# A trunk layer on one core: w_up's right operands without their zero columns, first-half outputs written in two pieces, and the end of w_up in another order without GpSimd

## The chip, the core and the metric

The kernel runs on one core of a Trainium2 chip. The metric is the device time of one execution in microseconds (us), from the first to the last instruction with what the launch adds around them. Each kernel is run several times and the median counts. One further execution is recorded by the hardware profiler; rows and times within the kernel are from that one, counted from its first instruction.

## What is computed

One layer of a diffusion backbone for 128 context tokens and 512 latent tokens (640 in all), 1024 channels wide, in float32. Attention and a gated convolution are mixed, then follows a feed-forward part with a convolution over the tokens in its middle. The change lies in the feed-forward part:

```
def dwconv3(x, w):
    xp = jnp.pad(x, ((0, 0), (1, 1), (0, 0)))
    return w[0] * xp[:, :-2] + w[1] * xp[:, 1:-1] + w[2] * xp[:, 2:]

def conv_ffn(u, p):                       # u: (tokens, 1024), w_up: (1024, 2*2816), w_down: (2816, 1024)
    up = dwconv3(u @ p["w_up"], p["conv_ffn"])
    g, val = jnp.split(up, 2, axis=-1)
    return (jax.nn.silu(g) * val) @ p["w_down"]
```

Context and latent tokens are two separate sequences: the convolution sees a zero before the first and behind the last token of each.

## The kernel before, in words

**Products.** TensorE multiplies rounded operands (type fp32r). So that float32 accuracy is kept, each operand is cut in a high and a low part: ScalarE copies it to the rounded type (`hi_of`, line 1061, written as tile `whi`), VectorE subtracts that from the original (`lo_of`, line 1068, tile `wlo`). A product is three matmuls, high by high, high by low and low by high (`block`, line 1079, for w_up; `mm3`, lines 207 to 209, for w_down).

**w_up.** The 5632 columns of w_up are 44 blocks of 128: 22 blocks of g and 22 of val, the pair j being block j of each. One pair is a product of a 256 x 1024 matrix with the 1024 x 640 matrix u. The first two pairs (`NPLAIN` = 2) are computed plainly. The 20 others go through Winograd's form of Strassen's scheme with seven half-size products per pair (`strassen(j)`, line 1620): A11, A12, S2, S1, S3, S4, A22, each of 4 blocks of the inner dimension times three matmuls, 84 matmuls of 128 x 128 by 128 x `HALF`. The right operands are the quarters of u and sums of them, made once (tiles ZB0 to ZB2, ZT; `right_hi`, `right_lo`).

**The zero columns.** u is kept transposed, channels on partitions and tokens along the row, in two tiles UFa and UFb. A row has 644 columns (`NCOL`): a zero, 128 context tokens, a zero, 512 latent tokens, two zeros, so that the convolution can later read its neighbours from the product's row. Its halves, and so every matmul's moving operand in w_up, have 322 columns (`HALF`). GpSimd writes the zeros into UFa and UFb (six memsets, line 1381).

**Out of w_up.** A pair's sums come together in PSUM (two banks per pair, out of the ring 7, 0, 1) and are put into rows of a tile C: row `cg` of g, row `cv` of val. `copied` (line 1087, ScalarE, tiles p and u) takes a bank to SBUF; `added` (line 1090, VectorE) adds a bank to it and writes half a row of C; `last_copy` (line 1703, ScalarE) writes the last half. Three pairs later (`FLAG` = 3) the convolution runs on that row: `tap_mid` (line 1558, ScalarE) writes the middle tap into a row of tile Y, `taps_out` (line 1563, VectorE) adds the two outer taps to it, `silu` (1568, ScalarE), `gated` (1572, VectorE) multiplies g by val, `act_hi` (1578, ScalarE) and `act_lo` (1582) cut the result in ACTa and ACTb. Y has two pairs of rows; ACTa and ACTb have four slots.

**w_down.** Its first 512 output columns are summed within w_up's stage in banks 2 to 6, one block of 128 inner channels per pair (`down(k)`, line 1606, four pairs later), with weights in a tile WD of two blocks (`down_hi`, 1596, ScalarE; `down_lo`, 1600). The other 512 columns come behind w_up, with weights taken by `next_unit` (cut at lines 181 and 182) and the activations of the last four blocks straight from ACTa and ACTb (`again(i, ts)`, line 1932, i = 0 to 3 for k = 18 to 21); those of the 18 others were stored to memory and are fetched and cut again (`act_of`, tiles AFB, AHB, ALB).

**Order.** Each engine runs its instructions in the order in which the code issues them. Within `strassen(j)` that order is written out between the seven products. Behind the last pair stands a list by hand (lines 1942 to 1980) for w = 19, x = 20 and y = 21. TensorE's part of it is: `down(18)`, 15 matmuls of 512 columns; `again(0)` for two of the five token blocks, 6; `down(19)`, 15; the third block of `again(0)` and `again(1)`, 12; `down(20)`, 15; `again(2)`, 9; `down(21)`, 15; `again(3)`, 9; then the first half's sums are read out (`finish(0, t)`) and the other token blocks of `again` follow. With `late`, `down` runs all five token blocks with ACTa and WD's high part, then all with WD's low part, then all with ACTb (line 1618). At this end three low parts are GpSimd's: WD of `down(18)` and `down(19)` (within the last pair), ACTb of x, and one block of weights (`next_unit(G)`).

Of the kernel before, what the change touches and what calls it, by code (L numbers as in the profile page):

```python
# [11 lines left out]
F32 = mybir.dt.float32  # L12
F32R = mybir.dt.float32r
AF = mybir.ActivationFunctionType
# [3 lines left out]
D = 1024  # L18
KT = 8
NCTX = 128  # L20
# [5 lines left out]
DFF = 2816  # L26
NJ = DFF // 128
NCOL = 644
HALF = NCOL // 2
NACT = NCOL - 2  # L30
NRING = 4
FLAG = 3
# [75 lines left out]
def trunk_layer(ctx, tc, x_prompt, x_sample, cache_k, cache_v, c, c_ctx, w_ada, b_ada, g_pre1, g_post1, g_pre2,  # L108
# [1265 lines left out]
    TX = region(rb, "r4", [5, D], F32, "TX")  # L1374

    r7 = [rb.tile([128, n], F32, tag=f"r7{x}", name=f"UF{x}") for n, x in ((4 * NCOL, "a"), (3328, "b"))]
    UFS = [x[:, 0:4 * NCOL].rearrange("p (k c) -> p k c", c=NCOL) for x in r7]
    rows3 = r7[1][:, 4 * NCOL:4 * NCOL + 256].rearrange("p (i c) -> p i c", i=2)
    for a, b in ((0, 1), (NCTX + 1, NCTX + 2), (NCOL - 2, NCOL)):
        for x in UFS:  # L1380
            G.memset(x[:, :, a:b], 0.0)
# [89 lines left out]

    def modulated(t, hf):
        row = 1 if t == 0 else 0
        c0 = 1 if t == 0 else 2 + t * 128
# [33 lines left out]
    def crows(j):  # L1508
        if "c" not in room:
            room["c"] = region(ra, "r3", [7, NCOL], F32, "C")  # L1510
        return room["c"][:, j % 4, :], room["c"][:, 4 + j % 3, :]

    plain_out = {}

# [4 lines left out]
        block(plain_out[j, tok, i], (j, i), step, f"B{step + 1}{tok + 1}", step == 0, step == 1)  # L1519

    def plain_copy(j, tok, i):
        dst = crows(j)[i][:, tok * HALF:(tok + 1) * HALF]
        S.activation(dst, plain_out[j, tok, i], AF.Copy, scale=(1.0, -1.0)[i])

    def sums(j):

# [93 lines left out]
    def strassen(j):  # L1620

        f, nxt = j - FLAG, j + 1 if j + 1 < NJ else None
        g = NJ - FLAG if nxt is None else None
        cg, cv = crows(j)
        pair[j] = tuple(bank(n)[:, 0:HALF] for n in BANKS[j])
        if j > NPLAIN:
            last_copy(j - 1)
        else:
            plain_copy(1, 1, 1)
        if f >= 0:  # L1630
            tap_mid(f, 0)
        lo_of((j, 1))
        product(j, "A11")

        copied(j, "p1", 0)
        if f >= 0:
            tap_mid(f, 1)
            taps_out(f, 0, (0,))
        product(j, "A12")

        hi_of((j, 2), left(j, 2))
        added(cg[:, 0:HALF], j, "p1", 1)
        if f >= 0:
# [12 lines left out]
        if f >= 0:  # L1656
            gated(f)
        if nxt:
            adds = sums(nxt)
            adds[0]()  # L1660
        if g:
            cut_upto(len(state["cut"]) + 1)
            tap_mid(g, 0)
            tap_mid(g, 1)
        if j >= DLAG:
            down(j - DLAG)
        product(j, "S3")

        added(cv[:, HALF:], j, "p5", 0)
        lo_of((j, 3))  # L1670
        if nxt:
            pair_load(j + 2)
            hi_of((nxt, 0), left(nxt, 0))
            lo_of((nxt, 0))
            adds[1]()
        q = max((j - DLAG + 1) // 2, 0)
        if j == NPLAIN or (j > DLAG and (j - DLAG) % 2 == 1):
            down_hi(q)
            down_lo(q, G if g else V)
            down_load(q + 2 if q else 1)  # L1680
            if q == 0:
                down_load(2)
        if f >= 0:
            act_hi(f)
        if g:
            act_lo(f)
            taps_out(g, 0)
            silu(g)
        product(j, "S4")

        if nxt:
            hi_of((nxt, 1), left(nxt, 1))
        added(cg[:, HALF:], j, "u2", 1)
        if nxt:
            adds[2]()
        if g:
            taps_out(g, 1)
        elif f >= 0:
            act_lo(f)
        product(j, "A22")  # L1700

    def last_copy(j):
        S.activation(crows(j)[1][:, 0:HALF], pair[j][0], AF.Copy)


    for row in (1, 0):
# [61 lines left out]
    for t in range(1, NT + 1):  # L1768
        if t >= 2 and t != 4:
            normed(t - 2)  # L1770
        sq_b(t - 1)
        scaled(t - 1, 1)
        for k in (0, 1):
            if t < NT:
                wo_step(t, k)
        if t == NT:
            hi_of((1, 0), raws[1, 0])
            plain(0, 0, 0, 0)
        residual(t - 1)
# [12 lines left out]
        if t == 3:  # L1792
            right_hi("B11", "11", 0, 258)
            normed(2)
            right_lo("B11", "11", 0, 258)
        if t < NT:
            scaled(t, 0)
        if t == 3:
            right_hi("B21", "21", 0, 258)
        if t == 4:  # L1800
            right_hi("B11", "11", 258, HALF)
            right_lo("B11", "11", 258, HALF)
            right_lo("B21", "21", 0, 258)
            right_hi("B21", "21", 258, HALF)
            right_lo("B21", "21", 258, HALF)
        for k in range(3, KT):
            if t < NT:
                wo_step(t, k)
# [131 lines left out]
        bload(G2[:, row, :], 3, row)  # L1940
    w, x, y = NJ - 3, NJ - 2, NJ - 1
    us.append(state["cut"][state["next"]])
    gated(w)
    last_copy(y)
    act_hi(w)
    tap_mid(x, 0)
    down(NJ - 4)
    again(0, range(2))
    act_lo(w)
    tap_mid(x, 1)  # L1950
    taps_out(x, 0)
    tap_mid(y, 0)
    silu(x)
    taps_out(x, 1)
    tap_mid(y, 1)
    down(w, True)
    gated(x)
    down_hi(NJ // 2 - 1)
    act_hi(x)
    down_lo(NJ // 2 - 1)  # L1960
    act_lo(x, G)
    pms.append(bank(BANKS[NJ - 1][0]))
    again(0, (2,))
# [12 lines left out]
    down(y)  # L1976
    again(3, range(3))
    NU, tail, av = NJ // 2 - 2, 3, {}
    for t in range(NT):
# [47 lines left out]
```

## Time and profile before

| | us |
|---|---|
| median of 3 runs | 1115.15 (1114.73 to 1116.89) |
| the profiled execution, its own time | 1117.1 |
| its span, first to last instruction | 1115.3 |
| attention and what is ahead of the mixer's products | 0 to about 320 |
| the mixer's products by Strassen's scheme, 320 columns wide | about 320 to 555 |
| w_conv_out, w_o, second normalisation | about 555 to 669 |
| w_up, with half of w_down in it | 669.4 to 1013.5 |
| end of w_up: 96 matmuls from `down(18)` to `again(3)` | 1013.5 to 1040.7 |
| the rest of w_down | 1040.7 to 1109.0 |
| last residual and store | 1109.0 to 1115.3 |

How to read the views: "busy" of TensorE (PE) is modelled from pipelined matmuls, so matmul starts, not durations, tell its pace. A row of a timeline gives start, duration, engine, line, operation, operands as out<-in, and in brackets the idle time ahead of it with what ended it. PEclk is the TensorE clock that was granted, 1.00 being full speed.

### The profile page before, as it was taken

The page shows a single profiled execution, that of the slowest core. Times are in us where ns is not written, and L with a number is a line of the kernel's source. Part 1 is how long each engine was busy: PE and PEld are TensorE (multiplying, and loading weights), DVE is VectorE, ACT ScalarE, POOL GpSimd, SP SyncE. Part 2 cuts the span into 40 slices and gives each one's busy share as a digit, 9 for nine tenths or more (in the row PEclk, how much of TensorE's full clock was granted, in tenths as well). Part 3 has the DMA queues.
Part 4 walks back from the last instruction along what each step waited for, and adds up shares of the span by engine and source line. Part 5 has one row for each costly group of instructions (what it writes and reads, how often), then busy time and mean ns, then how long its engine had stood idle before and what let it go on. Part 6 is the DMA issues. An engine that isn't in the chain of part 4 may idle for free.

```text
span 1115.3 us, 20886 instructions
## 1 busy us (share of the span) xinstructions
PE 1082.4 (97%) x8581; PEld 999.5 (90%) x8581; DVE 815.6 (73%) x1211; ACT 567.5 (51%) x983; POOL 149.8 (13%) x194
## 2 busy tenths in 40 slices
PE   7999999988999999999999999999999999999997
PEld 5788877877999999999999889999999999997786
DVE  4578988785647889888555468888878877888544
ACT  5277677673335445454522365655546554555441
POOL 2056676640000000000000021000000000002001
PEclk9999999999999999999999999999999999999999
DMA  9683356341213223322332634333323332315722
GB/s 334 206 211 115 97 155 149 107 133 50 86 58 95 76 77 96 94 76 80 109 97 88 231 135 135 89 99 106 116 86 116 106 91 91 118 51 189 255 91 94
DMA packets 188989, 133.47 MB, mean 120 GB/s; under 512 B 16914, under 2 KB 171086, under 8 KB 188878
## 3 DMA queue, kind: packets, MB, share of 16 engines
q1 hardware_dynamic: 188782, 132.11, 39.1%
q8 instruction: 67, 1.10, 0.4%
q14 instruction: 28, 0.23, 0.1%
q10 hardware_dynamic: 112, 0.04, 0.0%
HBM read 120.01 MB, written 12.24 MB: 119 GB/s over the span
## 4 chain that ended last, share of the span: by engine, by line
PE 82%; DVE 7%; ACT 2%; issue 1%; POOL 0%; DVEq 0%; POOLq 0%; ACTq 0%
PE b L1079 46%; PE b L209 9%; PE b L207 9%; PE b L208 9%; PE s L852 2%; PE s L661 2%; DVE mx L804 1%; DVE PT L825 1%; DVE Y L1563 1%; PE s1b L852 1%; ACT pr L809 1%; PE s1a L207 1%; DVE PT L882 0%; PE s1b L207 0%; PE s1a L208 0%
## 5 line engine op out<-in xcount | busy, mean ns | idle before, releaser
L1079 PE MATMUL b<-ZB,whi 128*128 128x322 f32 x1024 | 228.5, 310 | 0.0
L1079 PEld LDWEIGHTS b<-ZB,whi 128*128 128x128 f32 x1024 | 173.8, 189 | 1.6
L1079 PE MATMUL b<-ZB,wlo 128*128 128x322 f32 x512 | 159.4, 311 | 0.0
L1079 PE MATMUL b<-MT,whi 128*128 128x320 f32 x608 | 134.1, 308 | 0.0
L1079 PEld LDWEIGHTS b<-MT,whi 128*128 128x128 f32 x608 | 101.6, 188 | 0.0
L1079 PEld LDWEIGHTS b<-ZB,wlo 128*128 128x128 f32 x512 | 96.2, 188 | 0.0
L1079 PE MATMUL b<-MT,wlo 128*128 128x320 f32 x304 | 93.8, 308 | 0.0
L1066 ACT ACTIVATE whi<-SUM 128x1024 fp32r<-128x1024 f32 x40 | 42.2, 1055 | 79.9 <-DVE SUM L1533 71.7
L1563 DVE SCALAR_TENSOR_TENSOR Y<-C,cffn,Y 128x642 f32<-128x642 f32 x88 | 81.0, 922 | 0.9
L182 DVE TENSOR_TENSOR wlo<-raw,whi 128x1024 fp32r<-128x1024 f32 (+1 forms) x31 | 33.6, 1085 | 53.3 <-ACT whi L181 52.8
L1079 PE MATMUL b<-UH,whi 128*128 128x320 f32 x228 | 70.5, 309 | 0.0
L1079 PE MATMUL b<-UL,whi 128*128 128x320 f32 x228 | 70.4, 309 | 0.0
L1079 PE MATMUL b<-UH,wlo 128*128 128x320 f32 x228 | 70.2, 308 | 0.0
L1070 DVE TENSOR_TENSOR wlo<-raw,whi 128x1024 fp32r<-128x1024 f32 (+1 forms) x51 | 50.4, 1020 | 25.3 <-ACT whi L1066 24.4
L1066 ACT ACTIVATE whi<-WB 128x1024 fp32r<-128x1024 f32 x38 | 40.1, 1056 | 54.9 <-DVE WB L1174 54.9
L1087 ACT ACTIVATE p<-b 128x322 f32<-128x322 f32 (+1 forms) x78 | 34.2, 439 | 57.9 <-PE b L1079 57.9
L1090 DVE TENSOR_TENSOR C<-b,p 128x322 f32<-128x322 f32 x40 | 19.7, 493 | 52.2 <-PE b L1079 51.8
L1079 PEld LDWEIGHTS b<-MT,wlo 128*128 128x128 f32 x304 | 57.0, 188 | 0.0
L1070 DVE TENSOR_TENSOR wlo<-WB,whi 128x1024 fp32r<-128x1024 f32 x38 | 46.5, 1223 | 8.9 <-ACT whi L1066 8.9
L1066 ACT ACTIVATE whi<-raw 128x1024 fp32r<-128x1024 f32 (+1 forms) x51 | 43.5, 892 | 18.2 <-PE b L209 9.8
L804 DVE TENSOR_REDUCE mx<-s 128x1 f32<-128x640 f32 x64 | 50.2, 811 | 3.3 <-PE s L661 3.0
L809 ACT ACTIVATE pr<-s,mx 128x640 f32<-128x640 f32 x56 | 44.1, 791 | 15.7 <-DVE mx L804 13.2
(400 smaller groups left out, 3096.8 us busy)
## 6 DMA issues: line engine op xcount, KB each, us to landing
raw<-in_w_in_dram SPq DMA_DIRECT2D x48, 512.0 KB, 3.8
RAW<-in_w_up_dram SPq DMA_DIRECT2D x40, 512.0 KB, 4.1
raw<-in_w_ada_dram SPq DMA_DIRECT2D x32, 512.0 KB, 4.4
raw<-in_w_down_dram SPq DMA_DIRECT2D x22, 512.0 KB, 3.9
actd<-Y SPq DMA_DIRECT2D x18, 321.0 KB, 2.6
AFB<-actd SPq DMA_DIRECT2D x18, 321.0 KB, 5.1
XT<-in_w_ada_dram SPq DMA_DIRECT2D x9, 512.0 KB, 5.9
raw<-in_w_conv_out_dram SPq DMA_DIRECT2D x9, 512.0 KB, 3.8
```

What stands on the lines that cost most here:

```text
L182: eng.tensor_tensor(out=lo[:, :n], in0=raw, in1=hi[:, :n].bitcast(F32), op=ALU.subtract)
L207: PE.matmul(out, ah, bh, start=start, stop=False)
L208: PE.matmul(out, ah, bl, start=False, stop=False)
L209: PE.matmul(out, al, bh, start=False, stop=stop)
L804: V.tensor_reduce(out=mx, in_=self.sc[h], axis=AX.X, op=ALU.max, negate=True)
L809: S.activation(self.pr[:, h, :], self.sc[h], AF.Exp, bias=mx, scale=rs, accum_out=self.sm[:, h:h + 1])
L852: PE.matmul(self.out(i, c % 2, 128, 384), VR[self.g][rows, c, :], PT[rows, s0:s0 + 4, :, 32 * c:32 * c + 32], start=n == 0, stop=n == 9, t ...
L1066: S.activation(to[0], raw, AF.Copy)
L1070: V.tensor_tensor(out=lo, in0=raw, in1=hi.bitcast(F32), op=ALU.subtract)
L1079: PE.matmul(out, p[:, ws], q[:, k, :], start=start and k == 0 and n == 0, stop=stop and k == 3 and n == 2, skip_group_check=True)
L1087: S.activation(t, pair[j][b], AF.Copy)
L1563: V.scalar_tensor_tensor(out=y, in0=crows(j)[i][:, d:d + NACT], scalar=cffn[:, 44 * d + o:44 * d + o + 1], in1=y, op0=ALU.mult, op1=ALU.add)
```

## The change

1. `HALF` is 320 in place of 322: u's rows hold the 640 tokens alone (`UFS`, `modulated`), and the six memsets on UFa and UFb go. Three memsets on C take their place, made once when C is first used (`crows`).
2. A row of C keeps its 644 columns with the zeros. Its first half now is tokens 0 to 319, which in C lie on either side of the zero between context and latent tokens: columns 1 to 128 and 130 to 321. So each write of a first half (`added` on `cg`, `last_copy` and `plain_copy`) becomes two instructions, of 128 and 192 columns (`into`, `filled`). The second half is one piece of 320.
3. In the last pair and behind it the order is new, and no low part is GpSimd's: WD, ACTb of x and the weights' low part go to VectorE. `down(y)` is `late` and comes ahead of `again(2)`. The outer taps of one row are issued apart (`taps_out(.., (0,))` and `(2,)`), with other work between them.

Not touched are the number of matmuls, the work on w_down's weights, and everything ahead of u's rows.

```
-HALF = NCOL // 2
+HALF = NTOK // 2
...
-    UFS = [x[:, 0:4 * NCOL].rearrange("p (k c) -> p k c", c=NCOL) for x in r7]
+    UFS = [x[:, 0:4 * NTOK].rearrange("p (k c) -> p k c", c=NTOK) for x in r7]
...
-    for a, b in ((0, 1), (NCTX + 1, NCTX + 2), (NCOL - 2, NCOL)):
-        for x in UFS:
-            G.memset(x[:, :, a:b], 0.0)
...
             room["c"] = region(ra, "r3", [7, NCOL], F32, "C")
+            for a, b in ((0, 1), (NCTX + 1, NCTX + 2), (NCOL - 2, NCOL)):
+                G.memset(room["c"][:, :, a:b], 0.0)
...
+    SIDES = (((0, NCTX, 1), (NCTX, HALF, 2)), ((0, HALF, HALF + 2),))
+
+    def into(row, side, f):
+        for a, b, c in SIDES[side]:
+            f(row[:, c + a:c + b], slice(a, b))
...
+    def filled(row, side, j, tag, b):
+        x = pair.pop((j, tag))
+        into(row, side, lambda dst, cs: V.tensor_tensor(out=dst, in0=pair[j][b][:, cs], in1=x[:, cs], op=ALU.add))
...
-        added(cg[:, 0:HALF], j, "p1", 1)
+        filled(cg, 0, j, "p1", 1)
...
-            down_lo(q, G if g else V)
+            down_lo(q)
...
+    tap_mid(x, 0)
     gated(w)
     last_copy(y)
+    taps_out(x, 0, (0,))
     act_hi(w)
-    tap_mid(x, 0)
+    tap_mid(x, 1)
     down(NJ - 4)
     again(0, range(2))
     act_lo(w)
-    tap_mid(x, 1)
-    taps_out(x, 0)
     tap_mid(y, 0)
+    taps_out(x, 0, (2,))
     silu(x)
     taps_out(x, 1)
     tap_mid(y, 1)
     down(w, True)
     gated(x)
+    act_hi(x)
+    taps_out(y, 0, (0,))
+    taps_out(y, 1, (0,))
     down_hi(NJ // 2 - 1)
-    act_hi(x)
     down_lo(NJ // 2 - 1)
-    act_lo(x, G)
+    taps_out(y, 0, (2,))
+    silu(y)
+    act_lo(x)
     pms.append(bank(BANKS[NJ - 1][0]))
     again(0, (2,))
-    next_unit(G)
-    taps_out(y, 0)
-    silu(y)
     again(1, range(3))
-    taps_out(y, 1)
+    taps_out(y, 1, (2,))
     down(x, True)
     gated(y)
+    next_unit()
     act_hi(y)
     act_lo(y)
     us.append(next_unit())
+    room["h"] = region(ra, "r3", [NT, D], F32, "HX")
+    down(y, True)
     again(2, range(3))
-    room["h"] = region(ra, "r3", [NT, D], F32, "HX")
-    down(y)
     again(3, range(3))
```

VectorE at the very end of w_up, before the change, from the last pair's sum of S4 (`C<-b,u`) on. Rows on Y from C are outer taps, `Y<-Y` is `gated`, ACTb is `act_lo`, WD is `down_lo`, L182 is the low part of weights:

```order
L1090 TENSOR_TENSOR C<-b_1223_10785,u_1227_10835 128x322
L1563 SCALAR_TENSOR_TENSOR Y<-C,cffn,Y 128x642 x2
L1572 TENSOR_TENSOR Y<-Y 128x642
L1582 TENSOR_TENSOR ACTb<-Y,ACTa 128x642
L1563 SCALAR_TENSOR_TENSOR Y<-C,cffn,Y 128x642 x4
L1572 TENSOR_TENSOR Y<-Y 128x642
L1600 TENSOR_TENSOR WD<-raw_10606,WD 128x1024
L1563 SCALAR_TENSOR_TENSOR Y<-C,cffn,Y 128x642 x4
L1572 TENSOR_TENSOR Y<-Y 128x642
L1582 TENSOR_TENSOR ACTb<-Y,ACTa 128x642
```

The same stretch of VectorE with the change, from x's last taps on:

```order
L1570 SCALAR_TENSOR_TENSOR Y<-C,cffn,Y 128x642 x3
L1579 TENSOR_TENSOR Y<-Y 128x642
L1570 SCALAR_TENSOR_TENSOR Y<-C,cffn,Y 128x642 x2
L1607 TENSOR_TENSOR WD<-raw_10642,WD 128x1024
L1570 SCALAR_TENSOR_TENSOR Y<-C,cffn,Y 128x642
L1589 TENSOR_TENSOR ACTb<-Y,ACTa 128x642
L1570 SCALAR_TENSOR_TENSOR Y<-C,cffn,Y 128x642
L1579 TENSOR_TENSOR Y<-Y 128x642
L182 TENSOR_TENSOR wlo_11075<-raw_10820,whi_11074 128x1024
L1589 TENSOR_TENSOR ACTb<-Y,ACTa 128x642
```

Two of y's four outer taps now stand ahead of WD's low part and two behind it; ACTb of x and the weights' low part, GpSimd's before, stand among them.

ScalarE at the same place before the change, from WD's high part for the last two blocks on (L1568 is `silu` of y, L181 weights' high parts, the ACTa rows are x's and y's):

```order
L1596 ACTIVATE WD<-raw_10606 128x1024
L1578 ACTIVATE ACTa<-Y 128x642
L181 ACTIVATE whi_11003<-raw_10782 128x1024
L1568 ACTIVATE Y<-Y 128x642
L1578 ACTIVATE ACTa<-Y 128x642
```

And with the change, from x's ACTa on:

```order
L1585 ACTIVATE ACTa<-Y 128x642
L1603 ACTIVATE WD<-raw_10642 128x1024
L1575 ACTIVATE Y<-Y 128x642
L181 ACTIVATE whi_11074<-raw_10820 128x1024
L1585 ACTIVATE ACTa<-Y 128x642
```

x's ACTa moved ahead of WD's high part, and y's `silu` ahead of the weights' high part.

TensorE behind `down(20)`, before the change (the first two rows are that block's last matmuls):

```order
L1618 MATMUL b_998_8393<-WD,ACTb 128x512
L1618 MATMUL b_999_8394<-WD,ACTb 128x512
L207 MATMUL b_1233_10934<-whi_11003,ACTa 128x512
L208 MATMUL b_1233_10934<-wlo_11004,ACTa 128x512
L209 MATMUL b_1233_10934<-whi_11003,ACTb 128x512
```

And with the change:

```order
L1625 MATMUL b_998_8399<-WD,ACTb 128x512
L1625 MATMUL b_999_8400<-WD,ACTb 128x512
L1625 MATMUL b_995_8396<-WD,ACTa 128x512
L1625 MATMUL b_996_8397<-WD,ACTa 128x512
L1625 MATMUL b_997_8398<-WD,ACTa 128x512
```

The nine matmuls of `again(2)` that stood between `down(20)` and `down(21)` now follow `down(21)`.

More of the change, by code (lines that the diff above doesn't have):

```diff
@@ L1521, in plain_copy @@
     def plain_copy(j, tok, i):
-        dst = crows(j)[i][:, tok * HALF:(tok + 1) * HALF]
-        S.activation(dst, plain_out[j, tok, i], AF.Copy, scale=(1.0, -1.0)[i])
+        into(crows(j)[i], tok, lambda dst, cs: S.activation(dst, plain_out[j, tok, i][:, cs], AF.Copy, scale=(1.0, -1.0)[i]))
+    def filled(row, side, j, tag, b):
+        x = pair.pop((j, tag))
+        into(row, side, lambda dst, cs: V.tensor_tensor(out=dst, in0=pair[j][b][:, cs], in1=x[:, cs], op=ALU.add))
     def sums(j):
@@ L1662, in strassen @@
             cut_upto(len(state["cut"]) + 1)
+            act_hi(f)
             tap_mid(g, 0)
-            tap_mid(g, 1)
+            act_lo(f)
+            taps_out(g, 0, (0,))
         if j >= DLAG:
@@ L1667, in strassen @@
         product(j, "S3")
-        added(cv[:, HALF:], j, "p5", 0)
+        filled(cv, 1, j, "p5", 0)
         lo_of((j, 3))
@@ L1682, in strassen @@
                 down_load(2)
-        if f >= 0:
+        if g:
+            tap_mid(g, 1)
+            taps_out(g, 0, (2,))
+            silu(g)
+            taps_out(g, 1, (0,))
+        elif f >= 0:
             act_hi(f)
[L1685 to L1688, printed above, removed]
         product(j, "S4")
@@ L1692, in strassen @@
             hi_of((nxt, 1), left(nxt, 1))
-        added(cg[:, HALF:], j, "u2", 1)
+        filled(cg, 1, j, "u2", 1)
         if nxt:
@@ L1696, in strassen @@
         if g:
-            taps_out(g, 1)
+            taps_out(g, 1, (2,))
         elif f >= 0:
@@ L1702, in last_copy @@
     def last_copy(j):
-        S.activation(crows(j)[1][:, 0:HALF], pair[j][0], AF.Copy)
+        into(crows(j)[1], 0, lambda dst, cs: S.activation(dst, pair[j][0][:, cs], AF.Copy))
     for row in (1, 0):
@@ L1792, in trunk_layer @@
         if t == 3:
-            right_hi("B11", "11", 0, 258)
+            right_hi("B11", "11", 0, 256)
             normed(2)
-            right_lo("B11", "11", 0, 258)
+            right_lo("B11", "11", 0, 256)
         if t < NT:
@@ L1798, in trunk_layer @@
         if t == 3:
-            right_hi("B21", "21", 0, 258)
+            right_hi("B21", "21", 0, 256)
         if t == 4:
[L1801 to L1805, printed above, removed]
+            right_hi("B11", "11", 256, HALF)
+            right_lo("B11", "11", 256, HALF)
+            right_lo("B21", "21", 0, 256)
+            right_hi("B21", "21", 256, HALF)
+            right_lo("B21", "21", 256, HALF)
         for k in range(3, KT):
```

2 lines of the change are left out of this document (1 added, 1 removed).

## The prediction

> **What bounds the kernel now.** I read the page first, then the chain of work that ended last, then starts.
>
> ```profile
> span 1115.3 us, 20886 instructions
> ...
> PE 1082.4 (97%) x8581; PEld 999.5 (90%) x8581; DVE 815.6 (73%) x1211; ACT 567.5 (51%) x983; POOL 149.8 (13%) x194
> ...
> PE 82%; DVE 7%; ACT 2%; issue 1%; POOL 0%; DVEq 0%; POOLq 0%; ACTq 0%
> ```
>
> TensorE carries the chain for 82% of the span. The busy times per stretch (columns PE, PEld, DVE, ACT, POOL, clock, DMA share, GB/s) say how sharply this holds in w_up:
>
> ```profile
> 736.00:1007.50 271.50, 271.50 (x1684) 260.09 (x1683) 222.31 (x280) 142.99 (x213) 0.00 (x0) 1.00 0.31 96
> ```
>
> In the steady pairs TensorE has no gap at full clock, VectorE is busy for 82% and ScalarE for 53%. So there only the pace of matmuls counts, and work added to the other two is free until it delays an operand. At the end of w_up this changes. The timeline of TensorE, start and duration first:
>
> ```profile
> 1007.52 0.46 PE L1079 MATMUL b<-ZB,whi 128*128 128x322 f32 x2
> ...
> 1011.88 0.42 PE L1079 MATMUL b<-ZT,wlo 128*128 128x322 f32 x1 [0.30 <-DVE wlo L1070]
> ...
> 1021.92 0.39 PE L207 MATMUL b<-whi,ACTa 128*128 128x512 f32 x1
> ...
> 1028.94 0.50 PE L208 MATMUL b<-wlo,ACTa 128*128 128x512 f32 x1 [0.33 <-POOL wlo L182]
> ...
> 1033.04 0.50 PE L207 MATMUL b<-WD,ACTa 128*128 128x512 f32 x1 [1.99 <-ACT ACTa L1578]
> ...
> 1035.12 0.63 PE L209 MATMUL b<-WD,ACTb 128*128 128x512 f32 x1
> ...
> 1040.68 0.39 PE L207 MATMUL b<-whi,ACTa 128*128 128x512 f32 x1
> ```
>
> Three waits stand here, the longest for ACTa of the last pair y. Behind it the clock falls:
>
> ```profile
> 1030.79:1034.20 3.41, 1.29 (x5) 0.59 (x4) 2.38 (x4) 1.69 (x2) 0.00 (x0) 1.00 0.54 147
> 1034.20:1037.62 3.42, 3.42 (x9) 2.65 (x9) 2.86 (x6) 2.52 (x6) 0.00 (x0) 0.50 1.01 401
> ```
>
> A stretch of 3.41 us in which TensorE was busy for 1.29 is followed by one at half clock.
>
> **The change, part by part: 320 columns.** The chain, in order of time (start, length, what), gives both paces:
>
> ```profile
> 369.92 185.09 PE b L1079 x1262
> ...
> 784.03 12.48 PE b L1079 x84
> 796.52 0.23 PE b L207
> ...
> 800.01 12.48 PE b L1079 x84
> ```
>
> The first row is the mixer, the same function with operands of 320 columns: 185.09 / 1262 = 146.7 ns per matmul. A pair in w_up: 12.48 / 84 = 148.6 ns with 322. The gap of 1.9 ns is more than the share of two columns, 148.6 x 2/322 = 0.9 ns. What the other 1.0 ns is the rows don't say; I take it that it goes with the row length, since function, engines and clock are the same, and VectorE is about as busy. w_up has 20 x 84 + 16 x 12 = 1872 such matmuls; the largest of their groups:
>
> ```profile
> L1079 PE MATMUL b<-ZB,whi 128*128 128x322 f32 x1024 | 228.5, 310 | 0.0
> ```
>
> Gain: 1872 x 1.9 ns = 3.6 us; lower end 1872 x 0.9 ns = 1.7 us; none would need 320 columns to run slower in w_up than in the mixer.
>
> The Trainium skill, "TensorE: Matmul & The Clock Gate", section "Wait — 56ns, not 53.3ns?", puts warm matmuls at N / 2.4 GHz plus 2.5 ns from start to start. Two columns would then be 0.83 ns and this term an estimated 1.6 us in place of 3.6; both measured paces lie some 11 ns above the rule, so I don't go by it.
>
> **Two pieces and memsets.** The groups of the steady pairs (736 to 1007), and ScalarE's and GpSimd's of the whole run (the numbers behind the bar: busy us, mean ns; then idle before):
>
> ```profile
> L1563 DVE SCALAR_TENSOR_TENSOR Y<-C,cffn,Y 128x642 f32<-128x642 f32 x68 | 60.1, 884 | 0.6
> L1090 DVE TENSOR_TENSOR C<-b,p 128x322 f32<-128x322 f32 x34 | 16.7, 493 | 47.0 <-PE b L1079 47.0
> L1572 DVE TENSOR_TENSOR Y<-Y 128x642 f32<-128x642 f32 x17 | 14.1, 829 | 1.8
> L1582 DVE TENSOR_TENSOR ACTb<-Y,ACTa 128x642 fp32r<-128x642 f32 x17 | 14.0, 823 | 0.0
> L1070 DVE TENSOR_TENSOR wlo<-RAW,whi 128x512 fp32r<-128x512 f32 x17 | 11.6, 681 | 0.0
> L1600 DVE TENSOR_TENSOR WD<-raw,WD 128x1024 fp32r<-128x1024 f32 x8 | 9.8, 1220 | 0.0
> ```
>
> ```profile
> L1578 ACT ACTIVATE ACTa<-Y 128x642 fp32r<-128x642 f32 x22 | 16.1, 734 | 5.2 <-DVE Y L1572 4.1
> L1596 ACT ACTIVATE WD<-raw 128x1024 fp32r<-128x1024 f32 x11 | 11.6, 1058 | 12.7 <-PE b L209 12.6
> L1703 ACT ACTIVATE C<-b 128x322 f32<-128x322 f32 x20 | 8.4, 422 | 0.0
> L1381 POOL MEMSET UFa<- 128x4 f32 x2 | 0.1, 106 | 333.2 <-issue 333.2
> ```
>
> From 512 to 1024 columns VectorE's subtraction rises by 539 ns, so about 140 ns of it do not depend on length. A second piece costs 0 to 0.14 us by that, at most a whole 0.49; I take 0.1 on VectorE, and on ScalarE 0 to 0.42 with 0.1 too. Per pair VectorE idles 47.0 / 17 = 2.8 us ahead of such additions, waiting for TensorE, and that hides it. The tightest follower is S1, which overwrites the bank that the two pieces read:
>
> ```profile
> 1000.75 0.49 DVE L1090 TENSOR_TENSOR C<-b,p 128x322 f32<-128x322 f32 x1 [0.64 <-PE b L1079]
> ```
>
> ```profile
> 1002.26 0.46 PE L1079 MATMUL b<-ZB,whi 128*128 128x322 f32 x2
> ```
>
> The addition ends at 1001.24, S1 starts at 1002.26: 1.0 us of cover. Behind the pieces on VectorE stand a tap and the low part for S3, which starts five microseconds later. Cost 0. The memsets, 0.1 us each, stand on an idle GpSimd, ahead of anything that reads C's zeros: 0.
>
> **The end.** From S3 of the last pair (1007.52) to the start behind `again(3)` (1040.68) 33.16 us pass. The 132 matmuls in it need 36 x 0.1486 + 96 x 0.2327 = 27.7 us, the latter pace being (800.01 - 796.52) / 15. So 5.5 us are lost to waits, restarts and half clock. What makes y late is seen on VectorE beside GpSimd:
>
> ```profile
> 1009.93 1.90 DVE L1070 TENSOR_TENSOR wlo<-RAW,whi 128x512 fp32r<-128x512 f32 x1
> ...
> 1024.41 6.88 DVE L1563 SCALAR_TENSOR_TENSOR Y<-C,cffn,Y 128x642 f32<-128x642 f32 x4
> ```
>
> ```profile
> 1008.85 2.43 POOL L1600 TENSOR_TENSOR WD<-raw,WD 128x1024 fp32r<-128x1024 f32 x1 [330.01 <-ACT WD L1596]
> 1024.21 1.73 POOL L1582 TENSOR_TENSOR ACTb<-Y,ACTa 128x642 fp32r<-128x642 f32 x1 [12.93 <-ACT ACTa L1578]
> 1025.90 2.98 POOL L182 TENSOR_TENSOR wlo<-raw,whi 128x1024 fp32r<-128x1024 f32 x1
> ```
>
> While GpSimd subtracts, 512 columns take VectorE 1.90 us in place of 0.68, and four taps 6.88 in place of 3.5. Without it VectorE saves 1.2 + 3.3 = 4.5 us and takes over WD (1.22), ACTb (0.82) and weights (1.22), of which only the first two stand ahead of y's ACTa, the weights after its gate.
>
> Now the new order from S3 on. S3 to A22 end at 1007.5 + 36 x 0.147 = 1012.8; A22's low part starts at 1009.9 and is there at 1010.6, before its first use at 1011.3, so the first wait goes. `down(18)` and six more run to 1017.7. VectorE meanwhile: WD 1.2, two taps 1.8, addition 0.5, tap 0.9, gate 0.8, from 1010.6 to 1015.8; ACTa of w by 1016.6, in time for `down(19)` at 1017.7. That ends at 1021.2. By then VectorE has done a tap, ACTb of w, three taps and x's gate (0.9 + 0.8 + 2.6 + 0.8, to 1021); y's first two taps follow (1.8, to 1022.7).
>
> From 1021.2 on two strings run side by side. TensorE: 12 + 15 matmuls, to 1027.5, then it needs y's ACTa. The others: WD's high part must wait until `down(19)` has read WD (0.2), then 1.06; WD's low part 1.22; tap 0.88; ACTb of x 0.82; tap 0.88; gate 0.83; ACTa 0.73: 6.6 us, to 1027.8; counted from 1022.7, when VectorE is free by the sums above, 1028.1. `again(2)`, 2.1 us of cover before, now stands behind. So a wait of 0.3 to 0.6 us is left, too short for the half clock, since 2.8 us of a stretch stay busy. I take 0.5 with 0.1 of restart. ACTb of y comes two instructions later (weights 1.22, then 0.82), at 1029.2, used 10 matmuls into `down(21)`, at 1030.3. `finish` of all blocks now waits for `down(21)`'s last five matmuls; `again(2)` and `again(3)`, 4.2 us, cover it. Gain 5.5 - 0.6 = **4.9 us**; at best 5.5.
>
> Sum: 3.6 + 4.9 = 8.5 us. The profiled execution (1117.1 with a span of 1115.3) would become 1108.6 with 1106.8. It stands 1.95 above the median of the three runs; I take the difference off the median: 1115.15 - 8.5 = 1106.65, said as **1106.7**.
>
> **Rivals.**
> - *Only two columns' worth* of pace: 1.7 in place of 3.6, so 1108.6. For it: nothing in the rows names the other 1.0 ns. Against it: 1262 matmuls of the mixer at 146.7. Chance 0.13. The rule above, 1.6 us, ends at much the same time.
> - *The wait for y stays long.* The two strings are near equal; if the second is later by 1.4 us, the wait is the 2 us of before and a half clock follows, 3.4 us at half pace, 1.7 lost. The end then gives 4.9 - 1.4 - 1.7 = 1.8, in all 5.4: 1109.8. It needs each of seven steps to be 0.2 us longer than its row says. Chance 0.10. The Trainium skill, same page, "Part 1: The HAM clock gate", has the clock fall after an idle window of about 3.4 us; here 2.1 idle of 3.41 were enough, so the row decides. By the rule this case would lose the wait alone.
> - *GpSimd isn't what slows VectorE* (the change doesn't do what it is said to): y's four taps keep their 3.3 us, all on the second string, and the half clock comes: the end gives 4.9 - 3.3 - 1.7 = -0.1, in all 3.5: 1111.7. Against it: the long instructions coincide with GpSimd's three. Chance 0.04.
> - *Slower:* the two pieces hold the bank and S1 waits in every pair. It begins where they end over 1.0 us later than one did; each further 0.1 us costs 20 x 0.1 = 2 us. To lose 2.2 us overall the pieces must take 0.49 + 1.0 + 0.54 = 2.0 us; at 2.2 us the time would be 1115.15 - 8.5 + 20 x 0.71 = 1120.9. The row of 0.49 speaks against it. Chance 0.03.
>
> **How the numbers follow.** Forecast 0.66, its own range 1105.9 to 1107.7 (no wait at all; a wait of 1.2). The remaining 0.04 are mixtures that leave less than 2.2 us. The range 1105.5 to 1110.0 takes in the first two rivals. About 0.2% (2.2 us) is what a measurement of this kernel can tell from no change: faster 0.93, same 0.04, slower 0.03.
>
> **What would show it.** Right: pairs of 84 matmuls in 12.32 us; no tap above 0.95 us in the last pairs; one wait of some 0.4 us ahead of `down(21)`; PEclk 1.00 until the last store. Wrong: 12.40 us per 84, a stretch at 0.50 behind 1027, or waits of TensorE for `C` within the pairs.

## The result, and the profile after

| | before | after |
|---|---|---|
| median, six runs each, before measured anew (us) | 1115.82 (1114.73 to 1118.29) | 1108.30 (1104.56 to 1109.73) |
| ratio | | 0.9924, 95% interval 0.9904 to 0.9945 |
| the profiled execution, its own time | 1117.1 | 1107.36 |
| its span | 1115.3 | 1105.6 |

The ratio is a gain of 8.5 us (6.1 to 10.7), which is what the prediction's sum gave; the median stands 1.6 us above the 1106.7 forecast, in the range. It also stands 0.6 us above the narrower range that the forecast's own mechanism was given (1105.9 to 1107.7) and next to the 1108.6 of the rival with two columns' share; the kernel before itself came out 0.7 us higher when measured anew, and between the two accounts the stages decide, not the median. The spread of 5 us among the runs follows the mean granted clock: the two shortest spans, 1102.8 and 1104.0 us, had 0.997, the two with 0.989 had 1107.6 and 1107.9.

The page of the changed kernel. TensorE does the same 8581 matmuls in 6.8 us less; its share of the chain of work is 83%, one point more.

```profile
span 1105.6 us, 20947 instructions
...
PE 1075.6 (97%) x8581; PEld 993.7 (90%) x8581; DVE 814.8 (74%) x1234; ACT 568.7 (51%) x1007; POOL 142.2 (13%) x188
...
PE 83%; DVE 5%; ACT 2%; issue 1%; POOL 0%; DVEq 0%; POOLq 0%; ACTq 0%
```

The chain in order of time (start, length, what): the mixer, and one of the pairs.

```profile
320.76 232.89 PE b L1079 x1596
...
797.54 12.31 PE b L1079 x84
```

A pair takes 12.31 us where it took 12.48: 146.5 ns a matmul, close to the 146.7 of the mixer before, as forecast (12.32). The mixer has changed too, which was not forecast; this is its row in the chain of before:

```profile
320.94 234.07 PE b L1079 x1596
```

In the steady pairs (same columns of the view as in the prediction) TensorE still has no gap and GpSimd no instruction; VectorE's share went from 82% to 83%:

```profile
731.00:1002.80 271.80, 271.80 (x1698) 259.70 (x1697) 225.98 (x301) 146.38 (x234) 0.00 (x0) 1.00 0.31 97
```

The groups of those pairs show the two pieces (mean ns behind the bar). 291 + 349 ns stand where one piece took 493, and VectorE still waits 4.8 us in 17 pairs ahead of the first piece and 38.3 us ahead of the other half's:

```profile
L1530 DVE TENSOR_TENSOR C<-b,p 128x320 f32<-128x320 f32 x17 | 8.4, 492 | 38.3 <-PE b L1079 38.3
L1530 DVE TENSOR_TENSOR C<-b,p 128x192 f32<-128x192 f32 x17 | 5.9, 349 | 0.0
L1530 DVE TENSOR_TENSOR C<-b,p 128x128 f32<-128x128 f32 x17 | 4.9, 291 | 4.8 <-PE b L1079 4.8
```

The end, TensorE's timeline from S3 of the last pair to the start behind `again(3)`:

```profile
1002.82 0.46 PE L1079 MATMUL b<-ZB,whi 128*128 128x320 f32 x2
...
1021.56 1.33 PE L1625 MATMUL b<-WD,ACTb 128*128 128x512 f32 x5
1023.07 2.59 PE L1625 MATMUL b<-WD,ACTa 128*128 128x512 f32 x10 [0.18 <-ACT ACTa L1585]
...
1030.83 0.39 PE L207 MATMUL b<-whi,ACTa 128*128 128x512 f32 x1
```

Of the three waits one is left. It stands in the bracket with 0.18 us; by the starts it is more, since five matmuls from 1021.56 at 0.2327 us would let the next start at 1022.72, and it starts at 1023.07, 0.35 us later. The stretches around it stay at full clock (the number behind POOL's count is PEclk):

```profile
1019.60:1023.00 3.40, 3.29 (x15) 2.30 (x13) 3.30 (x5) 2.42 (x4) 0.00 (x0) 1.00 0.72 173
1023.00:1026.40 3.40, 3.33 (x14) 2.74 (x15) 2.25 (x3) 1.44 (x3) 0.00 (x0) 1.00 0.94 359
1026.40:1029.80 3.40, 3.40 (x16) 2.76 (x15) 3.15 (x7) 3.40 (x11) 0.00 (x0) 1.00 1.03 413
```

VectorE there, without GpSimd beside it: 512 columns in 0.68 us where they took 1.90, WD's low part in 1.2, two taps in 1.68.

```profile
1005.18 0.68 DVE L1070 TENSOR_TENSOR wlo<-RAW,whi 128x512 fp32r<-128x512 f32 x1
1005.78 1.22 DVE L1607 TENSOR_TENSOR WD<-raw,WD 128x1024 fp32r<-128x1024 f32 x1
1006.92 1.68 DVE L1570 SCALAR_TENSOR_TENSOR Y<-C,cffn,Y 128x642 f32<-128x642 f32 x2
...
1017.75 1.23 DVE L1607 TENSOR_TENSOR WD<-raw,WD 128x1024 fp32r<-128x1024 f32 x1 [0.34 <-ACT WD L1603]
```

By these anchors the profiled executions differ like this (us):

| stage | before | after | change |
|---|---|---|---|
| start to the mixer's first product | 320.78 | 320.60 | -0.18 |
| mixer, first to last product | 233.92 | 232.75 | -1.17 |
| from there to S3 of the last pair (1007.52; 1002.82) | 452.82 | 449.47 | -3.35 |
| S3 to the start behind `again(3)` | 33.16 | 28.01 | -5.15 |
| from there to the end | 74.63 | 74.75 | +0.12 |
| span | 1115.31 | 1105.58 | -9.73 |

### The profile page after: what moved, and what is told of

It is laid out like the page before. It is cut to its first block, busy times and chain, and to the rows that moved or that the text cites. A ratio compares the mean times of both kernels' runs of the same rounds, so it can differ in the third digit from the quotient of the medians.

```text
span 1105.6 us, 20947 instructions
## 1 busy us (share of the span) xinstructions
PE 1075.6 (97%) x8581; PEld 993.7 (90%) x8581; DVE 814.8 (74%) x1234; ACT 568.7 (51%) x1007; POOL 142.2 (13%) x188
## 4 chain that ended last, share of the span: by engine, by line
PE 83%; DVE 5%; ACT 2%; issue 1%; POOL 0%; DVEq 0%; POOLq 0%; ACTq 0%
PE b L1079 45%; PE b L207 9%; PE b L209 9%; PE b L208 9%; PE s L852 3%; PE s L661 2%; DVE mx L804 1%; DVE PT L825 1%; ACT pr L809 1%; PE s1b L852 1%; PE b L1625 1%; PE s1a L207 1%; PE s1a L208 0%; PE s1a L209 0%; PE s1b L207 0%
## 5 line engine op out<-in xcount | busy, mean ns | idle before, releaser
L1079 PE MATMUL b<-ZB,whi 128*128 128x320 f32 x1024 | 225.9, 308 | 0.0
L1079 PE MATMUL b<-ZB,wlo 128*128 128x320 f32 x512 | 157.8, 308 | 0.0
L1570 DVE SCALAR_TENSOR_TENSOR Y<-C,cffn,Y 128x642 f32<-128x642 f32 x88 | 77.5, 884 | 0.7
L182 DVE TENSOR_TENSOR wlo<-raw,whi 128x1024 fp32r<-128x1024 f32 (+1 forms) x32 | 34.9, 1090 | 53.2 <-ACT whi L181 49.9
L1087 ACT ACTIVATE p<-b 128x320 f32<-128x320 f32 x78 | 34.1, 437 | 54.0 <-PE b L1079 52.2
L1530 DVE TENSOR_TENSOR C<-b,p 128x128 f32<-128x128 f32 (+2 forms) x60 | 20.9, 377 | 46.9 <-PE b L1079 46.0
```

What stands on the lines that cost most here:

```text
L182: eng.tensor_tensor(out=lo[:, :n], in0=raw, in1=hi[:, :n].bitcast(F32), op=ALU.subtract)
L1079: PE.matmul(out, p[:, ws], q[:, k, :], start=start and k == 0 and n == 0, stop=stop and k == 3 and n == 2, skip_group_check=True)
L1087: S.activation(t, pair[j][b], AF.Copy)
L1570: V.scalar_tensor_tensor(out=y, in0=crows(j)[i][:, d:d + NACT], scalar=cffn[:, 44 * d + o:44 * d + o + 1], in1=y, op0=ALU.mult, op1=ALU.add)
```

## The experiments

The short name **E** stands below for the time from S3 of the last pair to the start behind `again(3)`. A single run's time moves by some microseconds with the clock ahead of the mixer, so the stages are compared, and medians where several rounds were run.

**The two halves of the change, each alone.** The first kernel has part 1 and 2 (columns, pieces) with the order of before; the second has part 3 (order, no GpSimd) with 322 columns. The first, against the changed kernel:

```
-            down_lo(q)
+            down_lo(q, G if g else V)
...
-    act_lo(x)
+    act_lo(x, G)
...
+    next_unit(G)
+    taps_out(y, 0)
+    silu(y)
...
+    again(2, range(3))
...
-    down(y, True)
-    again(2, range(3))
+    down(y)
```

> The columns alone: 320 columns and the two pieces, with the old order at the end and GpSimd's three low parts. Theory (two separate terms): the pairs run at 146.6 ns per matmul, the stretch from the last pair's S3 to the matmul behind again(3) stays at 33.1 us, and the whole gains 3.6 us, ratio 0.9968. Rival (the columns alone make the end shorter too, because all that VectorE and ScalarE do there has two columns less): the stretch falls below 32 us and the gain is over 5 us. Rival (the pieces cost TensorE something): more than 146.9 ns, or waits for the bank ahead of S1.

The second, against the changed kernel:

```
-HALF = NTOK // 2
+HALF = NCOL // 2
...
-        filled(cg, 0, j, "p1", 1)
+        added(cg[:, 0:HALF], j, "p1", 1)
```

> The end alone: rows of 322 columns with zeros and one-piece writes as before, with the new order and no low part on GpSimd. Theory: 148.6 ns per matmul in the pairs, 28.1 us from S3 of the last pair to behind again(3) in place of 33.2, gain 5.0 us, ratio 0.9955. Rival (the end needs the shorter rows to come out even): over 29 us and a wait of over 1 us for y's ACTa.

The columns alone: 1112.39 against 1116.93, ratio 0.9959 (0.9945 to 0.9973), 146.55 ns a matmul in w_up, E 31.60. The order alone: 1112.0, ratio 0.9957 (0.994 to 0.9974), 148.61 ns, E 28.23 with no wait. So each half is worth about 4.7 us, and the product of the ratios, 0.9916, lies within the interval of the whole change, 0.9904 to 0.9945, as it should if they add. Of the first kernel's gain 1.2 us lie in the mixer (below), which its theory did not have. The first kernel keeps the three waits of before and the long taps:

```profile
1007.85 0.41 PE L1079 MATMUL b<-ZT,wlo 128*128 128x320 f32 x1 [0.36 <-DVE wlo L1070]
...
1024.88 0.50 PE L208 MATMUL b<-wlo,ACTa 128*128 128x512 f32 x1 [0.44 <-POOL wlo L182]
...
1029.00 0.50 PE L207 MATMUL b<-WD,ACTa 128*128 128x512 f32 x1 [1.99 <-ACT ACTa L1585]
```

Its longest wait is 1.99 us, the same as before the change; but the clock stays at 1.00 behind it, and E is 31.60 where it was 33.16. The theory's 33.1 did not hold; the rival's figure did, but not its reason, since the wait is no shorter and y's four taps are as long (6.87 us; 6.88 before). The stretch in question is read under the last pair of experiments.

**Which part of the end: order or GpSimd.** The changed kernel with the three low parts back on GpSimd:

```
-            down_lo(q)
+            down_lo(q, G if g else V)
...
-    act_lo(x)
+    act_lo(x, G)
...
-    next_unit()
+    next_unit(G)
```

> The changed kernel with its new order, but the same three low parts back on GpSimd (WD within the last pair, ACTb of x, the weights cut behind y's gate). Theory (GpSimd slows VectorE while both run): the 512-column subtraction takes 1.9 us again instead of 0.7, what VectorE runs beside ACTb of x is longer by 1 to 1.7 us, y's ACTa comes 0.5 to 1.5 us later, and the stretch from S3 to behind again(3) is 28.5 to 29.8 us, against 28.0. Rival (the order alone made the end short): 28.0 us, and no long instruction on VectorE.

The other corner, the order of before with all low parts on VectorE, is the kernel of columns alone with these three edits reversed.

> 320 columns and the old order, but the three low parts on VectorE. Theory (both count: without GpSimd y's four taps take 3.5 us again, but three low parts of 3.3 us in all now stand ahead of them): y's ACTa comes about 1 us earlier than in the old kernel, the wait ahead of down(21) is 0.5 to 1.5 us, no half clock, and the stretch from S3 to behind again(3) is 29 to 30.5 us. Rival (only GpSimd counts): 28.0 to 28.5 us. Rival (only the order counts): 33 us.

With the new order and GpSimd E is 28.41, 0.40 more than without and just below what the theory gave. With the old order and VectorE E is 30.03, as forecast. In the four corners, all at 320 columns:

| E (us) | low parts on GpSimd | on VectorE |
|---|---|---|
| old order | 31.60 | 30.03 |
| new order | 28.41 | 28.01 |

So the order is the larger part (2.0 to 3.2 us), and GpSimd costs 1.6 in the old order, 0.4 in the new. Which of the moves within the order counts was not tested. What the new order takes from GpSimd's harm is seen in the third kernel. Its VectorE, then its GpSimd:

```profile
1007.21 1.92 DVE L1070 TENSOR_TENSOR wlo<-RAW,whi 128x512 fp32r<-128x512 f32 x1
...
1020.49 1.58 DVE L1607 TENSOR_TENSOR WD<-raw,WD 128x1024 fp32r<-128x1024 f32 x1 [0.94 <-ACT WD L1603]
...
1025.40 2.35 DVE L1589 TENSOR_TENSOR ACTb<-Y,ACTa 128x642 fp32r<-128x642 f32 x1 [0.81 <-ACT ACTa L1585]
```

```profile
1006.18 2.40 POOL L1607 TENSOR_TENSOR WD<-raw,WD 128x1024 fp32r<-128x1024 f32 x1 [325.64 <-ACT WD L1603]
...
1018.81 2.17 POOL L1589 TENSOR_TENSOR ACTb<-Y,ACTa 128x642 fp32r<-128x642 f32 x1 [10.22 <-DMA G<-bct]
...
1024.66 2.40 POOL L182 TENSOR_TENSOR wlo<-raw,whi 128x1024 fp32r<-128x1024 f32 x1 [3.68 <-ACT whi L181]
```

VectorE's three are long exactly where GpSimd's three run, but y's taps stand between two of them (1.67 us for two), and the low part that the last one stretches is not needed until ten matmuls later. Only the first still costs a wait, 0.36 us ahead of A22; `down(21)` has none, although the theory had y's ACTa come 0.5 to 1.5 us later.

One more kernel gives GpSimd a single low part, the one that no matmul waited for:

```
-    act_lo(x)
+    act_lo(x, G)
```

> The changed kernel with ACTb of x alone given back to GpSimd, where it took 2.2 us with nothing of TensorE's waiting for it; WD and the weights' low part stay VectorE's. Theory (VectorE's string sets the wait of 0.35 us ahead of the last down): VectorE loses 0.82 us of that string, its taps beside GpSimd's 2.2 us grow by at most as much, the wait goes: 27.5 to 27.9 us from S3 of the last pair to the start behind again(3), in place of 28.0, and a median within 0.5 us of the changed kernel's, 0.992 of the time before. Rival (the shared port takes from VectorE what it saves): the wait grows to 0.8 to 1.5 us, 28.4 to 29.1 us there, 0.5 to 1 us more in all.

The ratio is 0.9924 (0.9906 to 0.9941), the changed kernel's own; E is 28.21, between the two forecasts. On VectorE WD's low part now takes 2.17 us, 0.94 more, while ACTb's 0.82 has left it:

```profile
1017.53 2.17 DVE L1607 TENSOR_TENSOR WD<-raw,WD 128x1024 fp32r<-128x1024 f32 x1 [0.34 <-ACT WD L1603]
```

```profile
1016.44 2.17 POOL L1589 TENSOR_TENSOR ACTb<-Y,ACTa 128x642 fp32r<-128x642 f32 x1 [338.14 <-PE b L1625]
```

The theory, that the string gets shorter, has fallen: the wait of 0.18 us in the brackets became 0.38. No kernel here was shown to be faster than the changed one.

**Why 322 columns cost 2.1 ns more.** Two kernels keep all else of the change. In one the rows stand 322 apart and 320 columns are read; in the other the rows stand 320 apart and 322 columns are read, two of them the next row's, whose sums nobody reads (so the length written to PSUM is 322 as well; the last row of a tile, one in 8 or 16, is read with 320).

```
-    ZB0 = ra.tile([128, 4, 4, HALF], F32R, tag="r0", name="ZB0")
+    ZB0 = ra.tile([128, 4, 4, 322], F32R, tag="r0", name="ZB0")
...
-        TT[i] = (z[:, a], z[:, a + 1])
+        TT[i] = (z[:, a, :, 0:HALF], z[:, a + 1, :, 0:HALF])
```

> The changed kernel with w_up's right operands still 320 columns long, but stored 322 columns apart (1288 bytes), as their rows were before. Theory (where a row starts sets the 1.0 ns beyond two columns' share): 147.6 ns per matmul in the pairs. Rival (the length of 322 sets it): 146.6 ns.

```
-                PE.matmul(out, p[:, ws], q[:, k, :], start=start and k == 0 and n == 0, stop=stop and k == 3 and n == 2,
+                    at = (row + 4 * (n == 1) + k) * HALF
+                    mv = flat[:, at:at + HALF + (2 if row + 4 * (n == 1) + k + 1 < rows else 0)]
+                    out = wide[:, 0:mv.shape[1]]
...
+                PE.matmul(out, p[:, ws], mv, start=start and k == 0 and n == 0, stop=stop and k == 3 and n == 2,
```

> The changed kernel with rows 320 columns apart, but the pairs' moving operands read 322 columns (two of the next row, whose products are not used; the last row of a tile, 4 of 84 matmuls, stays at 320). Theory (where a row starts): 147.5 ns per matmul, two columns' share of 0.9 ns alone. Rival (the length of 322): 148.5 ns.

A third is the second with 4 in place of the 2: 324 columns.

> The changed kernel with rows 320 apart, every w_up matmul of the seven products reading 324 columns (four of the next row's; the sums' four extra columns are not read, so the output stays). In question is why 322 columns cost 148.6 to 148.7 ns a matmul, 2.1 more than 320 (146.55), when 320 to 512 rises by (232.7 - 146.55) / 192 = 0.449 ns a column. Theory: the length counts in steps of four columns, so that 322 is paid like 324: here 146.55 + 4 x 0.449 = 148.3 to 148.7, the same as with 322. Rival: some fixed surcharge of 1.2 ns falls on every length that is no multiple of 64 or on every reading across a row's end: here 146.55 + 1.8 + 1.2 = 149.5.

The chains' rows of a pair, for these three in turn:

```profile
829.03 12.34 PE b L1079 x84
```

```profile
785.57 12.49 PE b L1087 x84
```

```profile
783.31 12.54 PE b L1087 x84
```

| columns read | rows apart | us per 84 | ns a matmul |
|---|---|---|---|
| 320 | 320 | 12.31 | 146.5 |
| 320 | 322 | 12.34 | 146.9 |
| 322 | 322 | 12.48 | 148.6 |
| 322 | 320 | 12.49 | 148.7 |
| 324 | 320 | 12.54 | 149.3 |

The length of the matmul makes the difference, not where rows start: the theory of the first kernel fell, the rival was right. Steps of four columns fell as well, since 324 is not paid like 322 (149.3, with 148.3 to 148.7 expected); nearer is the surcharge on top of the columns. By (232.7 - 146.55) / 192 = 0.449 ns a column, 322 would cost 147.45 and 324 148.35; 1.2 to 1.3 and 0.9 ns are left over. This takes the slope between 320 and 512 columns as even, which no run shows; what is left over is open.

**The mixer's 1.2 us.** In all kernels so far the mixer goes with the size of the tiles of u's quarters, made later in the same memory: 233.92 us with 322 (the kernel before, the order alone, rows 322 apart), 232.7 to 232.8 with 320. UH and UL, the high and the low part of the mixer's right operand, use the memory of the first and the second of these tiles. The largest difference lies in matmuls on UH with the weights' high part; their group in the mixer (window 321 to 553), before and after:

```profile
L1079 PE MATMUL b<-UH,whi 128*128 128x320 f32 x228 | 70.5, 309 | 0.0
```

```profile
L1079 PE MATMUL b<-UH,whi 128*128 128x320 f32 x227 | 69.1, 304 | 0.0
```

The mean of one fell from 309 to 304 ns; 228 x 5 ns = 1.1 us. (The expectations below give the same step from the start of such a matmul to the next one, on UL, as 147.1 and 142.1 ns. Rows of a timeline are rounded to 10 ns, so only the difference of some 5 ns counts.) Two kernels put 32 unused columns behind the first and behind the second of u's tiles:

```
-    ZB0 = ra.tile([128, 4, 4, HALF], F32R, tag="r0", name="ZB0")
+    ZB0 = ra.tile([128, 16 * HALF + 32], F32R, tag="r0", name="ZB0")[:, 0:16 * HALF].rearrange("p (a k c) -> p a k c", a=4, k=4)
```

> The changed kernel with 32 unused columns (128 bytes per partition) behind the first tile of u's quarters, which stands in the memory of the mixer's UH: so UL and all that is allocated behind it start 128 bytes later, as they did before the change; nothing else differs. Theory (where UL stands sets the pace of the mixer's matmuls that go from UH to UL): these matmuls go from 142.1 to 147.1 ns, the mixer from 232.75 to 233.9 us, w_up stays at 146.55. Rival (the two columns of every row, not the place, did it in some other way): all stays as in the changed kernel.

```
-    ZB1 = ra.tile([128, 4, 4, HALF], F32R, tag="r1", name="ZB1")
+    ZB1 = ra.tile([128, 16 * HALF + 32], F32R, tag="r1", name="ZB1")[:, 0:16 * HALF].rearrange("p (a k c) -> p a k c", a=4, k=4)
```

> The same 32 unused columns behind the second tile, which stands in the memory of UL: UH and UL stay where they are in the changed kernel, and what is allocated behind UL starts 128 bytes later. Theory (UL's place relative to UH counts): the mixer stays at 232.75 us and 142.1 ns. Rival (the place of something behind it counts, weights or sums of operands): 233.9 us and 147.1 ns, as before the change.

Both texts give the shift as 128 bytes; it is 64. The first tile's memory is as large as the largest tile that uses it: before the change u's tile of 16 rows of 322 columns, 20608 bytes per partition; after it AHB of w_down's rest, 8 rows of 642 columns or 20544 bytes, since u's tile is now smaller (20480). The 32 columns make it 20608 again. The same holds for the second tile's memory, with ALB. So with the first shift UL and all that is allocated behind it start 64 bytes later than in the changed kernel: UL where it was before the change, the tiles behind it still 64 bytes or more ahead of where they were. With the second, UL stays and all behind it starts 64 bytes later. Between these two kernels only UL's memory stands elsewhere.

Their mixers in the chain:

```profile
320.57 234.09 PE b L1079 x1596
```

```profile
321.32 233.63 PE b L1079 x1596
```

The first shift gives back all 1.2 us (233.95 from first to last product; that group's mean is 309 ns again) and 0.2 ns per matmul in w_up; the second, which leaves UH and UL in place, gives back 0.74 of them (233.49; 307 ns). So the place of tiles in memory does it, with nothing else changed: 64 bytes on all that stands behind UL are worth 0.74 us, the same on UL another 0.46. Neither theory covers the second. Which of the tiles behind UL count, and why a place counts, is open.

**How much wait the end bears.** Products of 1024 columns without use, on VectorE ahead of y's `gated`, delay y's ACTa; with two:

```
+    V.tensor_tensor(out=EX[:, 4, :], in0=G2[:, 0, :], in1=G2[:, 1, :], op=ALU.mult)
+    V.tensor_tensor(out=EX[:, 4, :], in0=G2[:, 0, :], in1=G2[:, 1, :], op=ALU.mult)
     gated(y)
```

> The changed kernel with two more VectorE products of 1024 columns (1.22 us each, their result is overwritten later) ahead of y's gate. Theory (the two strings behind down(19) are near equal, so y's delay goes straight to TensorE, and a wait of over half a clock stretch costs a half clock): a wait of 2.4 to 2.7 us ahead of down(21), one stretch of 3.41 us at half clock behind it unless the wait falls across two stretches, and 30.4 to 32.2 us from S3 to behind again(3). Rival (the clock falls only after a whole idle stretch of 3.41 us): the wait alone, 30.4 us. Rival (slack hides it): 28.0 us.

With one of the two lines:

> The changed kernel with one more VectorE product of 1024 columns (1.22 us, its result is overwritten later) ahead of y's gate. Theory: a wait of 1.2 to 1.5 us ahead of down(21), no half clock, and 29.2 us from S3 to behind again(3). Rival (any wait above 1 us costs a half clock): 30.9 us.

One makes the wait 1.12 us and E 28.95, 0.94 more than without. Two make it 2.38 and E 31.78, 2.83 more for the second: the wait's 1.26 and a stretch at half clock. The half clock came as expected, and E with two products; with one, E is 0.25 us shorter than expected, and both waits are a little shorter.

```profile
1024.60 2.59 PE L1625 MATMUL b<-WD,ACTa 128*128 128x512 f32 x10 [1.12 <-ACT ACTa L1585]
```

```profile
1025.60 4.15 PE L1625 MATMUL b<-WD,ACTa 128*128 128x512 f32 x10 [2.38 <-ACT ACTa L1585]
```

The stretch ahead of the half clock and the one in it, with two products:

```profile
1022.50:1025.91 3.41, 1.03 (x5) 0.53 (x4) 3.38 (x5) 1.10 (x2) 0.00 (x0) 1.00 0.91 296
1025.91:1029.33 3.42, 3.42 (x9) 2.67 (x8) 1.88 (x3) 0.59 (x1) 0.00 (x0) 0.50 1.02 413
```

And the kernel of columns alone, whose wait of 1.99 us was not followed by half clock:

```profile
1024.25:1027.66 3.41, 2.31 (x9) 1.43 (x8) 3.27 (x4) 0.74 (x1) 0.58 (x1) 1.00 0.00 0
1027.66:1031.08 3.42, 1.95 (x7) 1.33 (x8) 2.50 (x3) 2.36 (x4) 0.00 (x0) 1.00 0.83 249
```

These bounds are not free to choose. That kernel's half-clock stretches ahead of the mixer start at 85.59, 225.54 and 256.26 us: 41 and 9 times 3.413 us apart; the next one, behind its last matmul, starts at 1106.18, 299 steps of 3.4133 us from the first. Counted on by 276 such steps from the first, a bound falls at 1027.66, within the wait, which so is shared between two stretches, busy for 2.31 and 1.95 us. In the kernel before, whose half-clock stretches start at 85.30 and 1034.20, 278 steps apart, the same wait fell into one stretch, of which 1.29 us were busy. The same wait cost 1.5 us more in the one execution than in the other (33.16 - 31.60, less 36 x 2.0 ns for the columns). That the share decides is not shown sharply: ahead of the mixer a stretch busy for 1.94 of 3.41 us was followed by half clock (the changed kernel, from 169.62 us), and one busy for 1.95 was not (two products, from 169.15 us); the second stretch of the columns alone has 1.95 as well, so that it stayed at full clock may have been close.

## Why the prediction was right, point by point

- **Columns**, 3.6 us forecast: -3.35 up to S3, and a pair went from 12.48 to 12.31 us, 0.17 x 20 = 3.4. The reason given, that the unexplained 1.0 ns goes with the row length, holds in the sense of the matmul's length; the spacing of rows adds some 0.3 ns. The rival of two columns' share would have been 1.7.
- **Pieces and memsets**, 0: TensorE waits for no C in the pairs, and VectorE's idle time ahead of the additions, 38.3 + 4.8 us in 17 pairs, is 2.5 us a pair where it was 2.8. The two pieces cost VectorE 0.15 us more than one, and ScalarE 0.16 (0.1 was taken for each).
- **The end**, 4.9: 5.15 measured. The two strings came out nearly as worked out. From the end of `down(19)` (1016.46) TensorE's 27 matmuls end at 1022.72; the other string, WD's high part first, was put at 6.6 us and y's ACTa releases `down(21)` at 1023.07, 6.61 later. VectorE was done with y's first two taps at 1017.41, in time, so that the shorter of the two estimates of the wait counted: 0.35, with 0.3 to 0.6 forecast.
- **What the 4.9 contained.** 1.7 of it was the half clock behind y's wait (1.5 to 1.6 by the runs: 33.16 - 31.60 above, 2.83 - 1.26 with two products), taken as part of the kernel before. By the two executions compared above it goes with the wait's place within a stretch of 3.41 us: the columns alone showed E at 31.60 with all three waits and without it. How often the kernel before meets it, one profile cannot say. Against the end without it, the new end gains 31.60 - 28.01 = 3.6. In an execution of before that is spared the half clock, the sum so is 3.4 + 3.6 + 1.2 = 8.2 us, in one that isn't 9.7; the measured ratio says 8.5.
- **Missed: the mixer.** Its code is not touched, and its 1.2 us was put at nothing without a term. The size of u's tiles moves what stands in memory. It touches the first term too: the pace of 146.7 ns, taken as that of 320 columns, is the mixer's 234.07 us / 1596, which became 232.89 / 1596 = 145.9 in the changed kernel. That the sum came out at the measured 8.5 is in part luck: it holds the half clock's 1.7 us, which need not fall, and lacks the mixer's 1.2, and an interval of 6.1 to 10.7 cannot tell 8.2 from 9.7.
- **GpSimd.** That its three low parts lengthen VectorE's instructions was right, row by row. As the cause of the end's loss it was given too much: of the 3.6 us GpSimd accounts for 0.4 to 1.6 and the order for 2.0 to 3.2, by which of them is taken first. The row of four long taps, named as what makes y late, showed only a part of it.
- The sign that PEclk would be 1.00 until the last store holds from the mixer to the last matmul. The profile of after has half-clock stretches at 9, 19, 88 and 173 us, in the part that the change doesn't touch, and from 1101.45 us on, behind the last matmul and while the last rows are stored, where it costs nothing.

## What to carry to other kernels

Zeros that only a later stage needs belong into that stage's rows and not into a moving operand: each column that TensorE reads is paid in every matmul (here 0.45 ns, and about 1 ns more with 322 or 324 columns), while two writes in place of one are free on an engine that waits anyway. A wait near 2 us on TensorE is best priced with two values, without and with a half-clock stretch behind it, and shortened by moving what stands in front of the waiting operand rather than by moving work to GpSimd. When tile sizes change, compare the stages that were not edited as well.

## What the runs showed of the hardware

- **The clock looks at stretches of 3.41 us that run on by themselves.** Those of which TensorE was busy for 0.30 (two products) and 0.38 (the kernel before) were followed by one at half clock; 0.57 (columns alone) was not. The Trainium skill, "TensorE: Matmul & The Clock Gate", section "What's actually happening", has windows of 3413 ns that don't start with the kernel, and the trace agrees (41 and 9 steps of 3.413 us); it puts half clock behind an idle window, while here a window that was busy for a third was enough. Where the bound lies is open: the stretches of 1.94 and 1.95 us above went either way.
- **VectorE's subtractions stand still beside GpSimd's.** Four times an instruction of VectorE was longer than alone by nearly the time that it overlapped GpSimd's: 1.24 us longer for 1.37 of overlap (512 columns), 0.35 for 0.49 (WD), 1.53 for 1.66 (ACTb), all with three low parts on GpSimd, and 0.94 for 1.08 with one. The Trainium skill, "SBUF — State Buffer", section "SBUF: two separate sides", calls the port that both use an exclusive lock, held for a whole instruction, by which the other one blocks, where VectorE's instruction has two inputs in SBUF; these subtractions have two, and their rows agree. Four taps in a row of the kernel before, also with two, were 3.35 us longer (6.88 for 3.53) beside 4.47 us of GpSimd's, so there less than the whole overlap was lost.
- **A matmul's pace depends on lengths and places:** 320, 322 and 324 columns took 146.5, 148.6 to 148.7 and 149.3 ns, and a shift of tiles by 64 bytes per partition moved the mixer's 1596 matmuls from 232.75 to 233.95 us. The cause of neither is known.
